# The first block of a transformer layer: first modulation sum on TensorE, the later ones in pairs on VectorE, with fixed orders

## The chip, the cores and the metric

The kernel runs on one core of one Trainium2 chip. The metric is the device time of one execution in microseconds (us): 996.87 is the median of three runs of the kernel before (996.62 to 997.46). The core has a matrix engine (TensorE, PE), VectorE (DVE), ScalarE (ACT), GpSimd (POOL), and SyncE (SP), whose queue issues nearly all loads. Each engine works through its own list of instructions in order, and waits on semaphores for the others. Sums on the matrix engine are built in PSUM, which the kernel uses as eight buffers of 128 x 512 float32.

## The reference, cut to what matters

One layer on a sequence of 512 tokens with 1024 features. The change concerns its beginning, which normalizes the input, modulates it by a condition c, and multiplies it by w_in:

```
c_act = silu(c)
mod = c_act @ w_ada + b_ada                      # (6 * 1024)
sh_t, sc_t, gt_t, sh_f, sc_f, gt_f = split(mod, 6)
h = layer_norm(x) * (1 + sc_t) + sh_t            # (512, 1024)
p = h @ w_in                                     # the first columns here, more later
```

A rotary table, cos and sin of pos * freqs, is computed beside it. Pooling, latent attention, spatial gating, an output projection and a feed-forward part with a short convolution follow; the change leaves them alone.

## The kernel before, in words

Every product is made of three: each factor is split into a high part (float32r) and a rest (low), and hi*hi, hi*lo and lo*hi are added up in PSUM.

The head, from the start to the first gate of its own (tile pg), computes 704 columns of h @ w_in: 448 latent columns into four buffers (lat, one for each 128 tokens), and 256 gate columns into two (g0ps). It walks over the 1024 features in eight pieces j of 128, and each piece has this work:

- loads on SP's queue (first_loads, L238): four tiles ada of 128 x 512 with the weights of this piece's shift and scale, and the piece's rows of w_in in two parts (w0);
- the modulation sum (first_modulation, L247): eight blocks of 128 features of c, 256 columns each, weighted by c_act on DVE in eight operations and added up into acc (two halves of four blocks each);
- prepare (L388): ACT rounds w0 to its high part w0h, POOL subtracts for the low part w0l; four one-column matmuls (L403) with a vector of ones add acc over the partitions into pm, ACT adds the bias (md, L409); four transposes turn x (pt, L414); ACT scales and shifts pt to hTjh and, once more in full precision, hfull (L420, L421), POOL subtracts for hTjl (L422);
- first_columns (L427): twelve products into lat, and first_gates (L437): six into g0ps.

x is normalized first: statistics on DVE (x_stats), an inverse root on POOL (power), and scaling on ACT (x_norm). Three wide matmuls (warm, L305) on normalized x run ahead of the first sum. The angles of the rotary table are made on DVE at the start (angles), reduced in two rounds between the sums (reduce_angles, L207), and turned to sines on ACT (sines, L217), in the program's text behind the sum of the last piece. Two gates with their own weights wg (gate, L354) follow the head: load, wsplit on ACT and DVE (L86), 24 products each (L111 to L114).

The order on each engine is made by a scheduler from the program's text and its data; `tc.issue_after(ins)` keeps what is inside it behind an instruction in this order, without a wait on the chip. So the orders below are those of the built program. SP's queue has eight loads open at a time: each load's issue waits for the landing of the load eight places before it, ACT's three loads of constants (kst, posi, cols; cols holds c, the biases and other columns) counted in.

Of the kernel before, what the change touches and what calls it, by code (L numbers as in the profile page):

```python
# [15 lines left out]
P = 128  # L16
# [34 lines left out]
def trunk(ctx: ExitStack, tc: tile.TileContext, A, out):  # L51
# [74 lines left out]
    def power(dst, src, scale, eps, n):  # L126
# [4 lines left out]
        nc.gpsimd.tensor_tensor(out=dst, in0=t[:, :n], in1=neghalf[:, :n], op=ALU.pow)  # L131
# [31 lines left out]

    kst = const.tile([P, N_CONST], F32, name="kst")
    nc.scalar.dma_start(out=kst, in_=A["consts"])
    posi = const.tile([P, TT], I32, name="posi")
    nc.scalar.dma_start(out=posi, in_=A["pos"])
    cols = const.tile([P, N_COLS], F32, name="cols")
    nc.scalar.dma_start(out=cols, in_=A["cols"])
# [29 lines left out]
    def angles():  # L199
        posf = const.tile([P, TT], F32, name="posf")  # L200
        nc.vector.tensor_copy(out=posf, in_=posi)
        for t in range(TT):
            nc.vector.tensor_scalar_mul(
                out=ang[:, t, :], in0=kst[:, K_FREQ : K_FREQ + 32], scalar1=posf[:, t : t + 1]
            )

    def reduce_angles(step):  # L207
# [4 lines left out]
        for c2 in TWO_PI:  # L212
            nc.vector.scalar_tensor_tensor(
                out=ang, in0=kq, scalar=-c2, in1=ang, op0=ALU.mult, op1=ALU.add
            )

# [15 lines left out]
    angles()  # L232

    first_raw = {}
    first_acc = {}
    last_acc = []

    def first_loads(j):  # L238
        ada = [act_t(f"ada{j}_{q}", F32) for q in range(4)]
        for q in range(4):  # L240
            nc.sync.dma_start(out=ada[q], in_=A["ada1"][j, q])
        raw = [act_t(f"w0{j}{i}", F32) for i in range(2)]
        nc.sync.dma_start(out=raw[0][:, :NL], in_=A["w0"][j, :, :NL])
        nc.sync.dma_start(out=raw[1][:, :256], in_=A["w0"][j, :, NL:])
        return ada, raw

    def first_modulation(j):  # L247
        adas, first_raw[j] = loads.pop(j)
        acct = act_t(f"acc{j}", F32)
        acc = [acct[:, :256], acct[:, 256:]]  # L250
        with ExitStack() as order:
            for ins in last_acc:
                order.enter_context(tc.issue_after(ins))
            for q in range(4):
                ada = adas[q]
                for i in range(2):
                    k = 2 * q + i
                    src = ada[:, i * 256 : (i + 1) * 256]
                    if q == 0:
                        nc.vector.tensor_scalar_mul(out=acc[i], in0=src, scalar1=cact[:, k : k + 1])  # L260
                    else:
                        ins = nc.vector.scalar_tensor_tensor(
                            out=acc[i], in0=src, scalar=cact[:, k : k + 1], in1=acc[i],
                            op0=ALU.mult, op1=ALU.add,
                        )
        last_acc[:] = [ins.ins]
        first_acc[j] = acc

    loads = {j: first_loads(j) for j in range(2)}


# [9 lines left out]
    def x_scales(a, b):  # L281
        power(rsx[:, a:b, 0], mvx[:, a:b, 1], 1.0, LN_EPS, b - a)
        nc.vector.scalar_tensor_tensor(
# [4 lines left out]
    def x_norm(t, n):  # L288
        nc.scalar.activation(
            xs[t][n], xs[t][n], AF.Identity, bias=rsx[:, t, 1:2], scale=rsx[:, t, 0:1]  # L290
        )

    for t in range(TT):
        stats = x_stats(t)
        if t % 2:
            x_scales(t - 1, t + 1)
            for u in (t - 1, t):
                x_norm(u, 0)
    first_modulation(0)
    first_modulation(1)  # L300

    warm = ps("warm")

    for t in (0, 0, 1):
        nc.tensor.matmul(warm, ident, xs[t][0], start=True, stop=True)  # L305
# [7 lines left out]
    def late_norm():  # L313
        with after_split():
            for t in range(TT):
                x_norm(t, 1)
# [69 lines left out]
    split_done = []  # L386

    def prepare(j):  # L388
        raws = first_raw[j]
        acc = first_acc[j]  # L390
# [9 lines left out]
        pm = ps("pm")  # L400
        for i in range(2):
# [1026 lines left out]
```

## Time and profile before

| What | Value |
|---|---|
| median of three runs | 996.87 us (996.62 to 997.46) |
| the profiled execution, its own time | 998.22 us |
| its span, first to last instruction | 996.1 us |
| PE busy over the span | 962.3 us (97%) |
| first product of the head (L433) | 19.17 us after the start |
| first pg, the end of the head (L111) | 69.26 us |
| mean granted clock of PE | 0.988 |

The profile's rows read: start in us, duration in us, engine, line, operation, output<-inputs, shape and a count; in square brackets the idle time of the engine just before and who ended it. Rows of adjacent instructions of one line are merged (x4). A float32 matmul shows as two rows (passes), one of float32r or a transpose as one. Rows by stretch of time give, for each engine, the busy us and a count, then the clock granted to PE (1.00 is full), the share of the DMA engines in use, and GB/s. A row of waits says which engine and line waited for whom: total us, times, longest.

### The profile page before, as it was taken

Reading aid. Unit: us, or ns where it says so; the run is one execution under the profiler, and the core shown is the slowest. Engines: PE = TensorE matmul, PEld = TensorE weight load, DVE = VectorE, ACT = ScalarE, POOL = GpSimd, SP = SyncE. Lnnn points to the kernel's source line nnn. Section 1 sums busy time; section 2 is a strip of 40 time slices with the busy share of each in tenths; the row PEclk is TensorE's granted clock in tenths of the full one; section 3 lists DMA queues with packets and bytes.
Section 4 is the critical chain, followed back from the end, with each engine's and each line's share of the span. In section 5 each row is a group of like instructions: output and inputs, shape, how many; then the busy total and the mean of one; then the engine's idle time right before and its main releaser. Section 6 shows DMA issues by size and latency. Waiting matters only on the chain.

```text
span 996.1 us, 12225 instructions
## 1 busy us (share of the span) xinstructions
PE 962.3 (97%) x4530; PEld 801.6 (80%) x4530; DVE 595.4 (60%) x923; ACT 392.7 (39%) x656; POOL 310.5 (31%) x311
## 2 busy tenths in 40 slices
PE   4999999999999999999999998999999999999996
PEld 3878888888878888888888876898888888888885
DVE  6937666566676565565433477685655565732357
ACT  3555555543233322422332244554444444422121
POOL 3556110222350022200011756421111121666654
PEclk9989999999999999999999998999999999999999
DMA  9703111125444633363223272133333343343222
GB/s 341 267 30 96 48 59 52 57 100 175 132 133 159 202 125 92 110 225 117 82 85 105 84 243 97 43 107 127 112 120 125 108 137 96 96 137 106 85 85 84
DMA packets 45274, 119.18 MB, mean 120 GB/s; under 512 B 5280, under 2 KB 8736, under 8 KB 45216
## 3 DMA queue, kind: packets, MB, share of 16 engines
q1 hardware_dynamic: 44784, 118.25, 36.4%
q8 instruction: 35, 0.57, 0.2%
q10 hardware_dynamic: 432, 0.17, 0.1%
q14 instruction: 23, 0.19, 0.1%
HBM read 116.30 MB, written 2.10 MB: 119 GB/s over the span
## 4 chain that ended last, share of the span: by engine, by line
PE 82%; DMA 6%; DVE 5%; POOL 3%; issue 2%; ACT 1%; DVEq 0%; POOLq 0%; SPq 0%; ACTq 0%
PE pzu L112 7%; PE pzu L111 7%; PE pzu L114 7%; PE pg L111 4%; PE pg L112 4%; PE pg L114 4%; PE py L111 4%; PE py L114 4%; PE py L112 4%; PE pyd L1045 3%; PE pyd L1042 3%; PE pyd L1044 3%; PE pu L848 3%; PE pu L847 3%; PE pu L845 3%
## 5 line engine op out<-in xcount | busy, mean ns | idle before, releaser
L91 DVE TENSOR_TENSOR wupl<-wup,wuph 128x1024 fp32r<-128x1024 f32 x38 | 48.8, 1285 | 71.4 <-PE pzu L114 45.6
L1011 POOL TENSOR_TENSOR d<-d,gtfb 128x512 f32<-128x512 f32 x44 | 75.3, 1732 | 34.5 <-DMA d<-in_wdn 32.0
L1284 POOL TENSOR_TENSOR zc<-zc 128x512 f32<-128x512 f32 x22 | 29.7, 1349 | 175.4 <-ACT zc L1283 154.6
L378 POOL TENSOR_TENSOR mg<-mg,th 128x512 f32<-128x512 f32 x16 | 31.3, 1959 | 146.0 <-DVE th L375 146.0
L1016 DVE TENSOR_TENSOR dl<-d,dh 128x1024 fp32r<-128x1024 f32 x18 | 29.7, 1649 | 54.5 <-PE pyd L1042 51.2
L90 ACT CAST wuph<-wup 128x1024 fp32r<-128x1024 f32 x38 | 39.9, 1050 | 46.5 <-PE pzu L112 46.5
L91 DVE TENSOR_TENSOR wgl<-wg,wgh 128x1024 fp32r<-128x1024 f32 x22 | 26.9, 1222 | 49.3 <-ACT wgh L90 36.5
L90 ACT CAST wbh<-wb 128x1024 fp32r<-128x1024 f32 x24 | 25.2, 1050 | 71.2 <-PE py L112 54.3
L725 DVE SCALAR_TENSOR_TENSOR ada<-adar,cact,ada 128x512 f32<-128x512 f32 x56 | 49.8, 917 | 0.6 <-DMA adar<-in_ada 0.5
L1015 ACT CAST dh<-d 128x1024 fp32r<-128x1024 f32 x18 | 18.9, 1052 | 61.2 <-PE pyd L1045 37.2
L1266 ACT ACTIVATE zc<-pzu,cols 128x512 f32<-128x512 f32 x44 | 34.2, 779 | 21.6 <-PE pzu L114 16.9
L90 ACT CAST wgh<-wg 128x1024 fp32r<-128x1024 f32 x22 | 23.3, 1060 | 41.6 <-PE pg L112 26.4
L91 DVE TENSOR_TENSOR wsgl<-wsg,wsgh 128x1024 fp32r<-128x1024 f32 x16 | 19.6, 1225 | 32.2 <-ACT wsgh L90 26.4
L91 DVE TENSOR_TENSOR wbl<-wb,wbh 128x1024 fp32r<-128x1024 f32 x24 | 31.1, 1294 | 9.9 <-ACT wbh L90 5.5
L90 ACT CAST wsgh<-wsg 128x1024 fp32r<-128x1024 f32 x16 | 16.8, 1052 | 49.0 <-PE pu L848 44.3
L1269 DVE SCALAR_TENSOR_TENSOR zc<-pzu,cols,zc 128x511 f32<-128x511 f32 x44 | 32.6, 743 | 3.9 <-ACT zc L1266 3.9
L646 POOL TENSOR_SCALAR pe<-pe,mx 128x128 f32<-128x128 f32 (+3 forms) x32 | 17.0, 533 | 54.4 <-DVE mx L645 54.0
L1273 DVE SCALAR_TENSOR_TENSOR zc<-pzu,cols,zc 128x510 f32<-128x510 f32 x44 | 32.6, 745 | 0.8
L1011 POOL TENSOR_TENSOR o<-o,gttb 128x512 f32<-128x512 f32 x16 | 26.4, 1672 | 17.1 <-DMA o<-in_wo 15.5
L1283 ACT ACTIVATE zc<-zc 128x512 f32<-128x512 f32 x22 | 13.9, 631 | 42.7 <-DVE zc L1273 42.6
L375 DVE SCALAR_TENSOR_TENSOR th<-th,py 128x512 f32<-128x512 f32 x16 | 11.0, 685 | 32.7 <-PE py L114 32.7
L778 POOL TENSOR_TENSOR asum<-apad 128x527 f32<-128x527 f32 x8 | 12.2, 1522 | 56.7 <-ACT apad L773 29.8
(1423 smaller groups left out, 3176.9 us busy)
## 6 DMA issues: line engine op xcount, KB each, us to landing
wup<-in_wup SPq DMA_DIRECT2D x44, 512.0 KB, 3.6
adar<-in_ada SPq DMA_DIRECT2D x64, 256.0 KB, 3.8
wb<-in_wb SPq DMA_DIRECT2D x24, 512.0 KB, 3.6
wg<-in_wg SPq DMA_DIRECT2D x22, 512.0 KB, 3.5
d<-in_wdn SPq DMA_DIRECT2D x22, 512.0 KB, 3.5
ada<-in_ada SPq DMA_DIRECT2D x32, 256.0 KB, 5.0
wsg<-in_wsg SPq DMA_DIRECT2D x16, 512.0 KB, 3.6
wa<-in_wa SPq DMA_DIRECT2D x8, 512.0 KB, 3.6
```

Of the source, the lines that this page charges most:

```text
L90: nc.scalar.copy(out=hi[:, :n], in_=raw[:, :n])
L91: ins = nc.vector.tensor_tensor(out=lo[:, :n], in0=raw[:, :n], in1=f(hi[:, :n]), op=ALU.subtract)
L111: nc.tensor.matmul(o, wh[:, c], xl[k], start=k == 0, stop=False)
L112: nc.tensor.matmul(o, wh[:, c], xh[k], start=False, stop=False)
L114: nc.tensor.matmul(o, wl[:, c], xh[k], start=False, stop=k == KT - 1)
L378: nc.gpsimd.tensor_tensor(out=merged[m], in0=merged[m], in1=th, op=ALU.add)
L725: nc.vector.scalar_tensor_tensor(out=acc[n], in0=src, scalar=cact[:, k : k + 1], in1=acc[n], op0=ALU.mult, op1=ALU.add,)
L845: nc.tensor.matmul(pu[t], hh, wl[:, c], start=False, stop=k == KT - 1)
L1011: nc.gpsimd.tensor_tensor(out=raw[:, c], in0=raw[:, c], in1=gt[n], op=ALU.mult)
L1266: nc.scalar.activation(t, pz, AF.Identity, bias=cols[:, cc + 3 : cc + 4], scale=cols[:, cc + 2 : cc + 3])
L1269: nc.vector.scalar_tensor_tensor(out=t[:, 1:512], in0=pz[:, 0:511], scalar=cols[:, cc + 1 : cc + 2], in1=t[:, 1:512], op0=ALU.mult, op1=AL ...
L1273: nc.vector.scalar_tensor_tensor(out=t[:, 2:512], in0=pz[:, 0:510], scalar=cols[:, cc : cc + 1], in1=t[:, 2:512], op0=ALU.mult, op1=ALU.add,)
```

## The change

The order of the head's work is written out in full, and its work is dealt out anew:

- The pieces come in groups: 0, 1, and the pairs (2, 3), (4, 5), (6, 7). Pairs have a new layout of the ada weights (ada1p): eight tiles per pair, each with both pieces side by side, so that one DVE operation of 512 columns serves two pieces.
- Piece 0 isn't summed on DVE: sixteen one-column matmuls take the ada tiles as they land, with c_act as the column (raw_sums), into g0ps. Ahead of it and between its first tiles stand warm-up matmuls on cols (ten, then one and one), and one on x behind its transposes.
- Of the pair (2, 3), DVE sums six of eight rows; the last two go to PE as raw rows with c_act, four one-column matmuls more for each of the two pieces.
- Products are ordered as hi*hi, then hi*lo, for lat and g0ps; then the next piece's transposes and one-column matmuls; then lo*hi. Behind the first two, the w0 split of piece j + 2 comes after the last products of piece j.
- DVE's orders: x statistics, piece 1, the pairs, then angles and both reductions; the sines stand behind the last split. On x's third and fourth row tiles ACT first scales 128 columns only.
- All loads of the head come ahead of those for later weights (load, last_load), and ACT loads cols first, kst last.

PE at the start, before (x_76 and so on are row tiles of x, acc_174 is piece 0's sum):

```order
L305 MATMUL warm<-x_76,ident 128x512 x2
L305 MATMUL warm<-x_78,ident 128x512
L403 MATMUL pm<-ones,acc_174 128x1
L414 MATMUL pt<-ident,x_76 128x128
L414 MATMUL pt<-ident,x_78 128x128
L414 MATMUL pt<-ident,x_80 128x128
L414 MATMUL pt<-ident,x_82 128x128
L403 MATMUL pm<-ones,acc_174 128x1 x3
L433 MATMUL lat_196<-w0h,hT0h 128x448
```

And now, the first seven rows, in which ada_0_114 and ada_1_115 are the first two tiles of piece 0, and lat_180 is only written to keep PE at work:

```order
L451 MATMUL lat_180<-cols,ident 128x232 x10
L442 MATMUL g0ps_181<-cact,ada_0_114 128x1
L442 MATMUL g0ps_182<-cact,ada_0_114 128x1
L442 MATMUL g0ps_181<-cact,ada_0_114 128x1
L442 MATMUL g0ps_182<-cact,ada_0_114 128x1
L451 MATMUL lat_180<-cols,ident 128x232
L442 MATMUL g0ps_181<-cact,ada_1_115 128x1
```

Nothing of DVE or of x stands ahead of the sum any more; x comes in with the transposes behind the fourth tile. The next place is PE from the transposes of one step to the next step, before:

```order
L414 MATMUL pt<-ident,x_83 128x128
L435 MATMUL lat_196<-w0h,hT5l 128x448
L435 MATMUL lat_197<-w0h,hT5l 128x448
L435 MATMUL lat_198<-w0h,hT5l 128x448
L435 MATMUL lat_199<-w0h,hT5l 128x448
L104 MATMUL g0ps_200<-hT5l,w0h 128x512
L105 MATMUL g0ps_200<-hT5h,w0l 128x512
L106 MATMUL g0ps_200<-hT5h,w0h 128x512
L104 MATMUL g0ps_201<-hT5l,w0h 128x512
L105 MATMUL g0ps_201<-hT5h,w0l 128x512
L106 MATMUL g0ps_201<-hT5h,w0h 128x512
L403 MATMUL pm<-ones,acc_570 128x1 x4
```

And now, where acc_328 holds the sums of pieces 6 and 7:

```order
L459 MATMUL pt<-ident,x_83 128x128
L475 MATMUL pm<-ones,acc_328 128x1 x2
L508 MATMUL lat_177<-w0h,hT5l 128x448
L508 MATMUL lat_178<-w0h,hT5l 128x448
L508 MATMUL lat_179<-w0h,hT5l 128x448
L508 MATMUL lat_180<-w0h,hT5l 128x448
L513 MATMUL g0ps_181<-hT5l,w0h 128x512
L513 MATMUL g0ps_182<-hT5l,w0h 128x512
L508 MATMUL lat_177<-w0h,hT6h 128x448
```

Before, pm at the end of step 5 was that of piece 7, a step ahead; now it is that of piece 6, needed by the very next step, and six products lie between it and hT6h. Two matmuls serve it in place of four. Third, DVE from the sum of piece 6 to the angles, before:

```order
L260 TENSOR_SCALAR acc_506<-ada_0_494,cact 128x256 x2
L262 SCALAR_TENSOR_TENSOR acc_506<-ada_1_495,cact,acc_506 128x256 x2
L262 SCALAR_TENSOR_TENSOR acc_506<-ada_2_496,cact,acc_506 128x256 x2
L262 SCALAR_TENSOR_TENSOR acc_506<-ada_3_497,cact,acc_506 128x256 x2
L260 TENSOR_SCALAR acc_570<-ada_0_558,cact 128x256 x2
L262 SCALAR_TENSOR_TENSOR acc_570<-ada_1_559,cact,acc_570 128x256 x2
L262 SCALAR_TENSOR_TENSOR acc_570<-ada_2_560,cact,acc_570 128x256 x2
L262 SCALAR_TENSOR_TENSOR acc_570<-ada_3_561,cact,acc_570 128x256 x2
L208 TENSOR_SCALAR kq<-ang 128x128
```

And now:

```order
L291 TENSOR_SCALAR acc_328<-ada_0_288,cact 128x512
L293 SCALAR_TENSOR_TENSOR acc_328<-ada_1_289,cact,acc_328 128x512
L293 SCALAR_TENSOR_TENSOR acc_328<-ada_2_290,cact,acc_328 128x512
L293 SCALAR_TENSOR_TENSOR acc_328<-ada_3_291,cact,acc_328 128x512
L293 SCALAR_TENSOR_TENSOR acc_328<-ada_4_292,cact,acc_328 128x512
L293 SCALAR_TENSOR_TENSOR acc_328<-ada_5_293,cact,acc_328 128x512
L293 SCALAR_TENSOR_TENSOR acc_328<-ada_6_294,cact,acc_328 128x512
L293 SCALAR_TENSOR_TENSOR acc_328<-ada_7_295,cact,acc_328 128x512
L205 CAST posf<-posi 128x4
```

Eight operations of 512 columns stand where sixteen of 256 stood, and all work on angles is behind them. On ACT, the two sine operations moved from ahead of hT6h to behind hT7h and its copy, ahead of the first wgh cast; on SP, the two wg and the wqr load moved from behind piece 1's loads to behind piece 7's.

The diff, cut to its core:

```
 def load(src, n, name):
-        nc.sync.dma_start(out=raw[:, :n], in_=src)
+        with tc.issue_after(last_load[0]):
+            nc.sync.dma_start(out=raw[:, :n], in_=src)
...
+    GROUPS = ((0,), (1,), (2, 3), (4, 5), (6, 7))
+    RAW = (6, 7)
+    def first_modulation(g, k0=0, k1=KT):
...
+        for k in range(k0, k1):
+            if len(js) == 1:
+                src = adas[k // 2][:, (k % 2) * 256 : (k % 2 + 1) * 256]
+                acc = first_acc[js[0]][k % 2]
+            else:
+                src = adas[k]
+                acc = first_sum[g]
...
+    def raw_sums(q):
+        for k in (2 * q, 2 * q + 1):
+            for i in range(2):
+                o = (k % 2) * 256 + i * P
+                ins = nc.tensor.matmul(
+                    g0psum[i][:, 0:1], first_ada[0][q][:, o : o + P], cact[:, k : k + 1],
+                    start=k == 0, stop=k == KT - 1,
+                )
+        return ins
+    def warm_up(n, src):
+        for _ in range(n):
+            w = src.shape[1]
+            ins = nc.tensor.matmul(lat[3][:, :w], ident, src, start=True, stop=True)
+        return ins
...
+            for i in range(2):
+                parts = [(part, ones[:, 0:1]) for part in acc]
+                if j in GROUPS[2]:
+                    o = (j - GROUPS[2][0]) * 256
+                    parts += [(first_ada[2][k][:, o : o + 256], cact[:, k : k + 1]) for k in RAW]
...
+        else:
+            sums = [g0psum[i][:, 0:1] for i in range(2)]
+            on_tensor(warm_up, 10, cols[:, :232])
+            for q in range(4):
+                on_tensor(raw_sums, q)
+                if q < 2:
+                    on_tensor(warm_up, 1, cols[:, :232])
+            on_tensor(turn)
...
+    first_split(0)
+    prepare(0)
+    on_tensor(warm_up, 1, xs[1][0])
+    late_norm((2, 3), 0, P)
+    first_split(1)
+    for g in range(2, len(GROUPS)):
+        first_loads(g)
+    behind = (
+        (first_modulation, 2, 0, RAW[0]), (first_modulation, 3, 0, 4), (first_modulation, 3, 4),
+        (first_modulation, 4, 0, 4), (first_modulation, 4, 4),
+        (angles,), (reduce_angles, COARSE), (reduce_angles, 1.0),
+    )
+    for work in behind:
+        on_vector(*work)
     for j in range(KT):
         hh, hl = hT_hi[j], hT_lo[j]
         wh, wl = w0s[j]
+        on_tensor(first_products, j, (hh, hh), (wh, wl), j == 0, False)
+        if j + 1 < KT:
+            on_tensor(prepare, j + 1)
+        if j < 2:
+            late_norm((2 * j, 2 * j + 1), 1, 0)
+        on_tensor(first_products, j, (hl,), (wh,), False, j == KT - 1)
+        if j + 2 < KT:
+            first_split(j + 2)
+    with after_split():
+        sines()
```

on_vector and on_tensor run a piece of work behind the one before it on their engine, by issue_after; first_products is the former twelve and six products in the order told above.

More of the change, by code (lines that the diff above doesn't have):

```diff
@@ L236, in trunk @@
     last_acc = []
[L238 to L250, printed above, removed]
+    last_load = []
@@ L251, in first_modulation, with on_vector @@
+    def on_vector(work, *args):
         with ExitStack() as order:
-            for ins in last_acc:
+            for ins in vector_last:
                 order.enter_context(tc.issue_after(ins))
[L254 to L265, printed above, removed]
@@ L286, in x_scales, with x_norm, x_first @@
         )
-    def x_norm(t, n):
-        nc.scalar.activation(
-            xs[t][n], xs[t][n], AF.Identity, bias=rsx[:, t, 1:2], scale=rsx[:, t, 0:1]
-        )
[L293 to L305, printed above, removed]
+    def x_norm(t, n, a=0, b=512):
+        return nc.scalar.activation(
+            xs[t][n][:, a:b], xs[t][n][:, a:b], AF.Identity, bias=rsx[:, t, 1:2], scale=rsx[:, t, 0:1]
+        )
+    def x_first(h):
+        for t in (2 * h, 2 * h + 1):
+            ins = x_norm(t, 0, 0, P if h else 512)
+        return ins.ins
+    for t in range(3):
+        on_vector(x_stats, t)
+    on_vector(x_scales, 0, 2)
+    split_done = [x_first(0)]
+    on_vector(x_stats, 3)
+    on_vector(x_scales, 2, 4)
+    x_first(1)
+    split_done.append(last_power[0])
+    on_vector(first_modulation, 1)
     def after_split():
@@ L399, in prepare, with on_tensor @@
         w0s.append((wh, wl))
-        pm = ps("pm")
-        for i in range(2):
-            for part in range(2):
-                nc.tensor.matmul(
-                    pm[:, i : i + 1], acc[part][:, i * P : (i + 1) * P], ones[:, 0:1],
-                    start=part == 0, stop=part == 1,
-                )
+    tensor_last = []
+    def on_tensor(work, *args):
+        with ExitStack() as order:
+            for ins in tensor_last:
+                order.enter_context(tc.issue_after(ins))
+            tensor_last[:] = [work(*args).ins]
@@ L409, in prepare @@
             nc.scalar.activation(
-                md[:, i : i + 1], pm[:, i : i + 1], AF.Identity, bias=bmod[:, j, i : i + 1]
-            )
-        pt = ps("pt")
-        for t in range(TT):
-            nc.tensor.transpose(
-                pt[:, t * P : (t + 1) * P], xs[t][j // 4][:, (j % 4) * P : (j % 4 + 1) * P], ident
+                md[:, i : i + 1], sums[i], AF.Identity, bias=bmod[:, j, i : i + 1]
             )
@@ L425, in prepare, with first_products @@
         hT_lo.append(hl)
-    def first_columns(j):
+        return last_matmul
+    def first_products(j, lefts, rights, start, stop):
+        for n, (hh, w) in enumerate(zip(lefts, rights)):
+            for t in range(TT):
+                ts_ = slice(t * P, (t + 1) * P)
+                nc.tensor.matmul(
+                    lat[t][:, :NL], hh[:, ts_], w[:, :NL], start=start and n == 0, stop=stop
+                )
+            for m in range(2):
+                c = slice(NL + m * P, NL + (m + 1) * P)
+                ins = nc.tensor.matmul(g0psum[m], w[:, c], hh, start=start and n == 0, stop=stop)
+        return ins
```

123 lines of the change are left out of this document (77 added, 46 removed).

## The prediction

> **What bounds the kernel now.** I read the page first, then busy time by stage, then what TensorE (PE) waited for in the head, then the clock that it was granted there, then single steps. All times are us.
>
> ```profile
> span 996.1 us, 12225 instructions
> ```
>
> The head, which the change rebuilds, is the part up to 69.26, where the first gate of the second kind (tile pg) begins. Busy time by stage, then PE's own waits up to 75:
>
> ```profile
> 0.00:11.17 11.17, 0.00 (x1) 0.00 (x1) 6.45 (x20) 2.36 (x4) 2.02 (x11) 1.00 0.81 280
> 11.17:19.17 8.00, 6.69 (x18) 3.50 (x18) 6.95 (x17) 4.17 (x9) 3.18 (x4) 1.00 1.05 394
> 19.17:69.26 50.09, 46.23 (x229) 41.37 (x229) 36.02 (x67) 25.49 (x64) 26.27 (x26) 0.86 0.49 178
> 69.26:996.14 926.88, 909.36 (x4285) 756.74 (x4283) 545.97 (x820) 360.72 (x583) 279.00 (x271) 0.99 0.35 112
> ```
>
> ```profile
> PE lat L433 <- ACT hT6h L420: 2.0, 1, 2.0
> PE pm L403 <- DVE acc L262: 1.8, 1, 1.8
> ```
>
> After 69.26 PE is busy for 909.36 of 926.88: what comes later is PE's own work, and a head that ends earlier moves it forward as a whole. In the head 19.17 pass before the first product. Then 50.09 pass for the eight steps, of which PE is busy 46.23, but at a mean clock of 0.86. Two waits make most of the idle time: 1.8 for a sum of VectorE (DVE), and 2.0 for hT6h, which stands behind the sines on ScalarE (ACT). Where the clock was lost, window by window, and how much of each window the one-column matmuls of tile pm (L403) filled, in the second fence:
>
> ```profile
> 16.60:20.00 3.40, 2.09 (x17) 1.95 (x16) 2.93 (x8) 2.07 (x5) 0.28 (x2) 1.00 1.03 408
> 20.00:23.40 3.40, 3.40 (x15) 3.20 (x14) 1.44 (x3) 0.55 (x3) 2.98 (x3) 0.50 1.04 385
> 33.70:37.10 3.40, 2.09 (x12) 1.69 (x11) 3.40 (x4) 1.85 (x6) 3.22 (x3) 1.00 1.06 382
> 54.10:57.50 3.40, 2.18 (x15) 1.84 (x13) 2.51 (x10) 1.07 (x4) 0.00 (x0) 1.00 0.00 0
> 57.50:60.90 3.40, 2.58 (x7) 2.32 (x8) 0.00 (x0) 2.51 (x7) 1.89 (x2) 0.51 0.03 5
> 60.90:64.40 3.50, 3.50 (x13) 3.04 (x12) 0.00 (x0) 1.45 (x2) 1.43 (x3) 0.50 0.00 0
> ```
>
> ```profile
> 16.60:20.00 3.40, 0.92 (x8) 0.86 (x7) 1.00 1.03 408
> 20.00:23.40 3.40, 1.70 (x8) 1.95 (x8) 0.50 1.04 385
> 54.10:57.50 3.40, 0.95 (x8) 1.05 (x8) 1.00 0.00 0
> ```
>
> The clock falls to 0.50 at 20.0 and at 57.5, after windows with 2.09 and 2.18 busy, but it holds after one with 2.09 busy (33.7 to 37.1). Without pm the three are 1.17, 1.23 and 2.09: one-column matmuls don't keep the clock. Nor do they bring it back: 20.0 to 23.4 is full, half of it with pm, and stays at 0.50. It came back at 26.8 and 64.4, each time after a window full of other matmuls. The two spells last 6.8 each and cost half of what PE does in them: 3.4 for the first, and 3.0 for the second, as PE restarts only at 58.3.
>
> **One step before, and what it costs after.** PE from step 4 to step 5, at full clock:
>
> ```profile
> 45.81 0.45 PE L433 MATMUL lat<-w0h,hT4h 128*128 128x448 f32 x1
> 47.53 0.60 PE L414 MATMUL pt<-ident,x 128*128 128x128 f32 x4
> 47.89 1.06 PE L435 MATMUL lat<-w0h,hT4l 128*128 128x448 f32 x4
> 48.78 0.40 PE L104 MATMUL g0ps<-hT4l,w0h 128*128 128x512 f32 x1
> 50.17 0.95 PE L403 MATMUL pm<-ones,acc 128*128 128x1 f32 x8
> 50.97 0.45 PE L433 MATMUL lat<-w0h,hT5h 128*128 128x448 f32 x1
> ```
>
> From start to start: eight products 1.72, four transposes 0.36, four products 0.89, six gate products 1.39, eight passes of pm 0.80, or 0.1 each. That is 3.95 to 4.0 of products per step, which the change orders anew and keeps. Its pm passes: 8 for piece 1 (two halves, two columns), 12 each for pieces 2 and 3 (a sum and two raw rows), 4 each for 4 to 7: 48 passes, 4.8. Before, the seven pieces after the first took 56, 5.6.
>
> The products with hTl now cover the way from pm over md to the next hTh. How long that way is shows the start of the head:
>
> ```profile
> 11.17 5.49 PE L305 MATMUL warm<-x,ident 128*128 128x512 f32 x6 [11.17 <-ACT x L289]
> 17.13 0.73 PE L403 MATMUL pm<-ones,acc 128*128 128x1 f32 x6
> 17.89 0.41 ACT L409 ACTIVATE md<-pm,bmod 128x1 f32<-128x1 f32 x2 [3.20 <-PE pm L403]
> 18.34 0.78 ACT L420 ACTIVATE hT0h<-pt,md 128x512 fp32r<-128x512 f32 x1
> 19.17 0.47 PE L433 MATMUL lat<-w0h,hT0h 128*128 128x448 f32 x1 [1.31 <-ACT hT0h L420]
> ```
>
> From the end of pm (17.86) to the first product (19.17) 1.31 pass, and pm ends about 0.15 after the next matmul could start (its last pass is 0.25 long, they follow at 0.1): 1.46. The cover is four products and two gate products, 0.89 + 0.46 = 1.35. So each step gains a new wait of 0.1; seven of them, 0.8. Sum for the steps: 8 × 3.95 + 7 × 0.36 + 4.8 + 0.8 = 39.7 against 50.1, so **−10.4**, with the clock at full rate.
>
> **The start.** The first sum no longer passes through DVE. What it then waits for are its four tiles, cols, and PE's own warm-up. The rows are the loads of constants, and SP's issues; each issue waits for the landing of the load eight places ahead, so they tell when earlier tiles had landed:
>
> ```profile
> 0.79 0.41 ACTq L165 DMA_DIRECT2D kst<-in_consts  x1
> cols<-in_cols ACTq DMA_DIRECT2D x1, 117.5 KB, 4.7
> kst<-in_consts ACTq DMA_DIRECT2D x1, 48.0 KB, 3.2
> 10.08 1.68 SPq L241 DMA_DIRECT2D ada<-in_ada  x3
> 12.78 0.33 SPq L244 DMA_DIRECT2D w<-in_w  x1
> 17.44 0.43 SPq L243 DMA_DIRECT2D w<-in_w  x1
> ```
>
> Cols is now issued at 0.79, and lands between 4.0 (with kst's 3.2) and 5.5 (with its own 4.7, for 117.5 KB); I take 4.8, nearer to its own row. The change orders the rest: ten warm-ups of 232 columns. A 512-column pass took 0.86 in the row of warm (six in 5.49, the tail included), so 232 columns take 0.39, and a warm-up of two passes 0.78, at the low rate; pm's passes went from 0.2 to 0.1 with the clock, so I take half of it, 0.39, once the clock is granted. Windows of 3.4 leave a grant between 8.2 and 11.6, in this profile's phase at 9.8: 6.4 warm-ups by then, the rest by 11.2. Then come four batches of 8 passes (0.8 each) and two warm-ups between them (0.39 each): 15.2. The second tile of piece 0 had landed by 11.4 (last of the three issues at 10.08), the fourth by 12.78, so PE sets this end. With 0.15, then md, hT0h and their gaps (1.31) the first product starts at 16.6: **−2.6**. The extremes: 14.9 if the tiles alone bound it (12.78 + 0.8 + 1.31), and 18 if the clock is granted last.
>
> The window before the first product then holds one of the small warm-ups (0.36 of it), four transposes (0.36) and the last, 512 columns wide (0.85): 1.6 without one-column matmuls. That lies between the 1.23 after which the clock fell and the 2.09 after which it held. If it falls, PE works without a break at half rate for one window, and loses 1.7. Where the windows lie isn't set by the program, so I count half: **+0.8**.
>
> The Trainium skill bears on both sides of this. "TensorE: Matmul & The Clock Gate", part 1, lets the clock drop after an idle window of about 3.4 us; by it none drops here, and the sum below would be 0.8 better. This trace disagrees: it fell at 57.5 with 2.18 of 3.40 busy. The same page, part 4, has transposes not count as busy; by it the window holds 1.2 and the clock falls each time, 0.9 worse than my sum. What this trace has on that is a window later on, all at 0.50 before it and at full clock right after, of which transposes (L1141) filled 2.78:
>
> ```profile
> 617.30:620.70 3.40, 2.78 (x12) 2.38 (x12) 0.50 0.00 0
> ```
>
> So the trace disagrees here too. Transposes stay in my count.
>
> **DVE and the loads.** The pieces from 2 on are summed by operations of 512 columns, two pieces at once. Here are DVE's eight operations for one piece before, and the same operation 512 wide in a later stage:
>
> ```profile
> 48.66 0.60 DVE L260 TENSOR_SCALAR acc<-ada,cact 128x256 f32<-128x256 f32 x2
> 49.19 4.86 DVE L262 SCALAR_TENSOR_TENSOR acc<-ada,cact,acc 128x256 f32<-128x256 f32 x6
> L725 DVE SCALAR_TENSOR_TENSOR ada<-adar,cact,ada x56: 741/746/1555, 232.4 to 803.8; 128x512 f32<-128x512 f32 x56
> ```
>
> The six took 4.86, 0.8 each, beside GpSimd's (POOL's) work on the same step. For 512 columns I take 1.05, nearer to the median of 0.75 than to the longest, 1.56. Loads run at 385 GB/s (the row from 20.0), 0.68 for 256 KB. Piece 1's last tile had landed by 17.44; the first pair's eight then land at 18.1 to 22.9, the next pair's by 30.2, the last's by 37.5, with the raw weights between them, and the three gate weights, moved behind, by 43. DVE is done with the pairs at 24.4, 33.9 and 42.3. PE asks for them (steps laid end to end from 16.6) at 24.8, 36.0 and 45.6: hidden, with 0.4 to spare on the first. If each took 1.56, they would be 2.7 late and then another 1.3 and 2.9, 6.9 in all; at 1.3, midway, only the first would be, by 1.1. The angles go behind on DVE, from 42 to 48, and the sines on ACT behind hT7, where PE has 3.95 of products left; they need 0.6, the wgh cast about 1.1 more. The gate weights aren't cast before 54, so landing by 43 is no wait.
>
> **The tail.** ACT's squares of lat begin 1.8 ahead of the first pg before; now the last lat product is 1.3 ahead of it, so this chain starts 0.9 later against PE:
>
> ```profile
> 67.49 0.38 ACT L469 ACTIVATE sq<-lat 128x256 f32<-128x256 f32 x1 [0.72 <-PE lat L435]
> 76.76 0.37 ACT L475 ACTIVATE cn<-lat,rr 128x128 f32<-128x128 f32 x1 [0.95 <-POOL rr L131]
> 80.15 1.47 PE L501 MATMUL ptc<-ident,cn 128*128 128x128 f32 x12
> ```
>
> Its last cn was done at 77.1, three before PE's transposes at 80.15. For the rotary part behind it on POOL, which I have no spare time for, I put **+0.2**, between 0 and 0.9.
>
> **The sum.** −2.6 − 10.4 + 0.8 + 0.2 = −12.0. The profiled execution took 998.22, so its like would take 986.2; it stands 1.35 above the median of the runs, 996.87. From the median, 984.9.
>
> **The rivals.**
> - The clock holds in every run. For it: the window from 33.7 held it with 1.3 idle. The 0.8 goes, and the waits of 0.1 may not show: 983.3 to 984.1.
> - A new wait takes part back: DVE under POOL at 1.3 to 1.56 per operation (1.1 to 6.9), or two windows at half clock in place of one (another 1.7, as both spells before lasted two). For it: the longest L725, and 0.4 to spare on the first pair; against it, DVE's mean in the head. 986.0 to 991.8.
> - No change: the rest of the kernel gives the gain back. Against it: its 17.5 of idle time would have to grow by 12, and nothing there is tied to the time since the start. 996.9.
> - Slower: the clock stays at 0.50 through the head, because the pm passes and new waits keep any window from being full (2.58 of 3.40 didn't do, 57.5 to 60.9). All 39.7 would double: 1024. It decides from 24 at half rate on. Against it: at half rate a step has products and transposes of 5.9 without a break, longer than a window, so most steps offer one.
>
> **Chances.** Forecast 0.54 (984.1 to 986.5), clock holds 0.18, new wait 0.23, no change 0.02, slower 0.03. The range goes from 982.3 (the clock holds, and the tiles alone bound the start: 984.1 - 1.7) to 989.0, midway through the new waits; no change, slower and the far end of the waits are left out. About 0.2% (2 us) is what a measurement of this kernel can tell from no change; the first three cases are all beyond it: faster 0.95, same 0.02, slower 0.03.
>
> **What would show it.** In the profile after: the first lat product near 16.6; first pg near 56 to 58; the clock at full rate from 21 at the latest up to pg; between steps PE idle 0.1 to 0.2 with hTh as the releaser; no PE wait for acc; no pm in front of a step that stands still. Wrong would be: a PE wait for acc over 1, a clock of 0.50 after 25, or a first product after 18.

## The result, and the profile after

| | us |
|---|---|
| before, median of 4 runs beside the changed kernel | 996.75 (995.59 to 997.46) |
| changed, median of 4 runs | **990.62** (990.05 to 991.69) |
| ratio, 95% interval | 0.9943 (0.993 to 0.9955) |
| forecast | 984.9 (982.3 to 989.0) |
| profiled execution: time, span, mean clock | 991.69, 989.7, 0.993 |

The change gains 6.1 where 12.0 was forecast, and the time lies outside the range. Where TensorE (PE) waited in the head and somewhat behind it, 0 to 75 (line numbers are the changed kernel's):

```profile
PE lat L451 <- DMA cols<-in_cols: 4.5, 1, 4.5
PE pm L475 <- DVE acc L293: 2.2, 1, 2.2
```

The first row is the start, before anything can run. The second is new: the two waits of before (sines, and a sum in another place) are gone, but PE now waits 2.2 for VectorE's (DVE's) sum of the first pair, pieces 2 and 3. The same place in order of time, from piece 0's first product on:

```profile
17.37 1.08 PE L508 MATMUL lat<-w0h,hT0h 128*128 128x448 f32 x4
...
22.57 1.08 PE L508 MATMUL lat<-w0h,hT1h 128*128 128x448 f32 x4
...
25.24 0.60 PE L459 MATMUL pt<-ident,x 128*128 128x128 f32 x4
28.09 0.35 PE L475 MATMUL pm<-ones,acc 128*128 128x1 f32 x2 [2.25 <-DVE acc L293]
...
30.88 1.86 PE L508 MATMUL lat<-w0h,hT2h 128*128 128x448 f32 x4
```

Piece 0 takes 5.20 from first product to first product. Piece 1 takes 8.31, 2.25 of it the wait. Piece 2 then begins at half speed: four products in 1.86 instead of 1.08. The clock by windows of 3.41, with the part behind the head as the last row; then how much of the first window the one-column passes of pm fill:

```profile
27.42:30.83 3.41, 2.74 (x18) 2.39 (x18) 3.27 (x6) 1.20 (x4) 0.00 (x0) 1.00 1.04 370
30.83:34.24 3.41, 3.41 (x10) 2.91 (x10) 3.30 (x4) 2.83 (x5) 2.66 (x2) 0.50 1.06 373
34.24:37.66 3.42, 3.42 (x25) 3.19 (x24) 3.35 (x4) 0.68 (x3) 1.86 (x2) 1.00 1.04 383
61.83:989.70 927.87, 910.15 (x4285) 757.07 (x4283) 542.83 (x820) 361.90 (x589) 279.24 (x273) 0.99 0.35 112
```

```profile
27.42:30.83 3.41, 1.47 (x12) 1.42 (x12) 0.41 (x2) 1.00 1.04 370
```

Of 2.74 busy in the first window, 1.47 are pm; 1.27 are other matmuls, and the next window is granted 0.50. The gate's products (tile pg), the end of the head, begin at 61.83 (69.26 before, 57.1 forecast); behind it 927.87 pass, where before took 926.88.

DVE over the same time:

```profile
15.11 1.53 DVE L291 TENSOR_SCALAR acc<-ada,cact 128x256 f32<-128x256 f32 x2 [2.09 <-DMA ada<-in_ada]
16.56 3.49 DVE L293 SCALAR_TENSOR_TENSOR acc<-ada,cact,acc 128x256 f32<-128x256 f32 x6
20.08 1.24 DVE L291 TENSOR_SCALAR acc<-ada,cact 128x512 f32<-128x512 f32 x1
21.36 6.58 DVE L293 SCALAR_TENSOR_TENSOR acc<-ada,cact,acc 128x512 f32<-128x512 f32 x5
27.86 0.47 DVE L291 TENSOR_SCALAR acc<-ada,cact 128x512 f32<-128x512 f32 x1
```

Piece 1's sum occupies it until 20.05, and the first pair's six operations (the third and fourth row) then take 7.9, until 27.94; the last row already belongs to the next pair. The forecast had them begin at 18.1 and end at 24.4.

### The profile page after: what moved, and what is told of

Its sections match the earlier page's. It is cut to its first block, busy times and chain, and to the rows that moved or that the text cites. A ratio compares the mean times of both kernels' runs of the same rounds, so it can differ in the third digit from the quotient of the medians.

```text
span 989.7 us, 12259 instructions
## 1 busy us (share of the span) xinstructions
PE 965.1 (98%) x4566; PEld 804.0 (81%) x4566; DVE 590.9 (60%) x889; ACT 393.5 (40%) x658; POOL 311.1 (31%) x311
## 4 chain that ended last, share of the span: by engine, by line
PE 83%; POOL 5%; DVE 5%; DMA 4%; issue 2%; ACT 2%; DVEq 0%; SPq 0%; POOLq 0%; ACTq 0%
PE pzu L113 7%; PE pzu L112 7%; PE pzu L115 7%; PE py L112 4%; PE py L115 4%; PE py L113 4%; PE pg L112 4%; PE pg L113 4%; PE pg L115 3%; PE pyd L1128 3%; PE pyd L1125 3%; PE pyd L1127 3%; PE pu L931 3%; PE pu L930 3%; PE pu L928 3%; PE lat L508 2%
## 5 line engine op out<-in xcount | busy, mean ns | idle before, releaser
L1094 POOL TENSOR_TENSOR o<-o,gttb 128x512 f32<-128x512 f32 x16 | 26.5, 1677 | 16.6 <-DMA o<-in_wo 15.0
```

The costliest lines, as they stand in the source:

```text
L1094: nc.gpsimd.tensor_tensor(out=raw[:, c], in0=raw[:, c], in1=gt[n], op=ALU.mult)
```

## The experiments

Theory A, from these rows: the first pair's sum is late on DVE, and wait and passes together then cost a window at half clock; about 3.9 (2.25 of waiting and 1.7 of clock). The ratios below are to the kernel before, measured beside each run. Rivals: the passes drop the clock whatever DVE does (B), what the head gains is given back behind it (C), the loss lies in the start.

**Fewer rows on DVE.**

```
-    RAW = (6, 7)
+    RAW = (4, 5, 6, 7)
```

> Theory A (the first pair's sum on VectorE ends late, TensorE waits 2.25 for it, and the window with that wait brings a stretch of 3.41 at half clock that costs 1.7): with four of the eight rows on TensorE, VectorE has two operations of 1.3 less and ends at 25.3, before TensorE asks at 25.8. The wait goes (-2.2), the half clock goes (-1.7), 16 more one-column passes cost 1.6: 988.3. Rival B (the one-column passes themselves drop the clock, the wait does not): the wait goes, the half clock stays, 16 passes are paid: 990.0. Rival C (what is gained there is given back behind the head): the head is 2.3 shorter, the time stays at 990.6.

990.35 (989.29 to 992.61, 6 runs), ratio 0.9937 (0.9924 to 0.9949). The wait is gone, and yet the clock fell at 30.49. The windows, then pm's part in the second and the fourth:

```profile
27.08:30.49 3.41, 3.41 (x29) 3.24 (x26) 3.30 (x4) 0.99 (x3) 1.52 (x2) 1.00 0.99 365
30.49:33.90 3.41, 3.41 (x10) 2.75 (x9) 3.30 (x4) 3.04 (x6) 1.89 (x2) 0.50 1.06 369
33.90:37.30 3.40, 3.40 (x28) 3.22 (x28) 3.33 (x4) 0.00 (x0) 1.68 (x2) 1.00 1.00 358
```

```profile
27.08:30.49 3.41, 2.29 (x20) 2.27 (x20) 0.41 (x2) 1.00 0.99 365
33.90:37.30 3.40, 2.02 (x19) 2.12 (x20) 0.00 (x0) 1.00 1.00 358
```

PE was busy for all of 27.08 to 30.49 and still lost the clock: 2.29 were one-column passes. That is B. A wait is not needed. The median fits B and C alike (990.0 and 990.6); it is the clock that decides.

**The wait filled.** Piece 2 only, ahead of its sums:

```
+            if j == 2:
+                for _ in range(5):
+                    nc.tensor.matmul(pm[:, 128:360], ident, cols[:, :232], start=True, stop=True)
```

> Five matmuls of 232 columns, whose result nothing reads, stand ahead of piece 2's sums and fill 2.0 of the 2.25 that TensorE waits there. Theory A (the wait drops the clock): no stretch of half clock at 30.8 to 34.2, so 1.7 less: 988.9, with the wait under 0.4. Rival B (the one-column passes drop it, or too few products in that window): the half clock stays, 990.6. Rival D (extra matmuls that come late hold up the sums): up to 0.5 more, 991.1.

989.8 (988.11 to 992.58, 6 runs), ratio 0.9933 (0.992 to 0.9947). No wait for pm and full clock from 18.33 through the head; the step of piece 2 takes 5.81 instead of 7.35. The gate's products are at 60.54, although this execution had lost a window at the start. With twelve passes and no idle time the clock holds, with twenty it did not. So A and B are one thing, the share of the window that is left for matmuls other than one-column passes. The time alone does not tell this run from the changed kernel: their intervals overlap.

**GpSimd's part.** The low halves of the weights of pieces 1 and 2 are left out, and the high half is multiplied in their place:

```
-                nc.gpsimd.tensor_tensor(
-                    out=wl[:, a:b], in0=raw[:, : b - a], in1=f(wh[:, a:b]), op=ALU.subtract
-                )
-        w0s.append((wh, wl))
+                if j not in (1, 2):
+                    nc.gpsimd.tensor_tensor(
+                        out=wl[:, a:b], in0=raw[:, : b - a], in1=f(wh[:, a:b]), op=ALU.subtract
+                    )
+        w0s.append((wh, wh if j in (1, 2) else wl))
```

> GpSimd's subtraction of the low half of the weights is left out for pieces 1 and 2 (two of 2.2 each); the high half is multiplied in its place, so the products have their number and shape. Theory A1 (GpSimd beside VectorE stretches VectorE's 512-wide operations from 0.75 to 1.3): the first pair ends at about 25.0, no wait of TensorE, no half clock: 990.6 - 2.2 - 1.7 = 986.7. Rival A2 (the first pair is late because it starts late, behind piece 1's sum at 20.05, or because its rows land late): its operations stay near 1.3 or wait for rows, the wait stays at 2.0 or more, 990.6.

989.02 (988.9 to 989.96, 5 runs), ratio 0.9925 (0.9913 to 0.9937). DVE's groups during the first pair's sum, in the changed kernel (20.0 to 27.9) and then here (18.1 to 23.6); the second number behind the bar is the mean of one in ns:

```profile
L293 DVE SCALAR_TENSOR_TENSOR acc<-ada,cact,acc 128x512 f32<-128x512 f32 x5 | 6.4, 1288 | 0.2
```

```profile
L293 DVE SCALAR_TENSOR_TENSOR acc<-ada,cact,acc 128x512 f32<-128x512 f32 x5 | 3.8, 752 | 0.2
```

The same five operations take 0.75 instead of 1.29 once GpSimd (POOL) does less beside them: A1. The pair is done at 23.5, 4.4 earlier. Of these, 2.5 are its own operations (7.86 before, 5.35 here). The other 1.9 are an earlier beginning, 18.15 instead of 20.08: piece 1's rows landed 0.9 earlier in this execution, and piece 1's sum, beside which GpSimd also does less, was 1.0 shorter. No wait and no half clock remain in the head, and the gate's products begin at 57.67; the forecast had 57.1. That is 4.2 earlier than in the first profile of the changed kernel. The spans of the two profiled executions differ by 2.5 (989.7 and 987.2), the medians by 1.6. So 1.6 of the 4.2 are lost again behind the head in these profiles. The waits up to 75 and PE behind the head:

```profile
PE ptk L597 <- POOL kr L575: 1.5, 1, 1.5
```

```profile
70.25 0.38 PE L601 MATMUL ptk<-ident,kr 128*64 128x128 f32 x2
72.14 0.33 PE L597 MATMUL ptk<-ident,kr 128*128 128x128 f32 x1 [1.51 <-POOL kr L575]
```

**The sines alone**, in the kernel before:

```
-                    if j + 2 == KT - 1:
-                        sines()
...
+    with after_split():
+        sines()
```

> The kernel before with one part of the change alone: the sine tables come behind the head's loop, all else as it was. If the forecast's reading of the kernel before holds (TensorE waits 2.0 at piece 7 behind ScalarE's sines and pays about 3.0 for the half clock that follows at 57.5 to 64.4): 996.75 - 5.0 = 991.8, and the stretch of half clock at 57.5 is gone. Rival: the wait goes and the clock drops all the same, because of the one-column passes: 994.7. Rival C: the sines then hold up the attention that follows and the time stays at 996.7.

994.74 (992.78 to 996.78, 12 runs), ratio 0.9981 (0.997 to 0.9992): 1.9 less, not 5. The wait of 2.0 and the half clock at 57.5 are gone, but the waits now have this, 1.8 before, and half clock follows at 39.8 for 3.41. The rival's 994.7 is met in number only, since its half clock at 57.5 is not there:

```profile
PE pm L403 <- DVE acc L262: 3.3, 1, 3.3
```

**Piece 2's columns first.** The same sum on DVE, in two column halves:

```
+                if half is not None:
+                    src = src[:, half * 256 : (half + 1) * 256]
+                    acc = acc[:, half * 256 : (half + 1) * 256]
...
-        (first_modulation, 2, 0, RAW[0]), (first_modulation, 3, 0, 4), (first_modulation, 3, 4),
+        (first_modulation, 2, 0, RAW[0], 0), (first_modulation, 2, 0, RAW[0], 1), (first_modulation, 3, 0, 4), (first_modulation, 3, 4),
```

> The changed kernel with the first pair's sum made in two column halves, piece 2's 256 columns first; TensorE's work is the same. Theory A: the six half operations for piece 2 end at 20.1 + 6 x 0.5 = 23.1, or at the last row's landing near 23, before TensorE asks at 25.2; the wait of 2.25 goes and no stretch of half clock follows it, so the first products of the gate are issued at 61.8 - 3.9 = 57.9, and the time is 990.6 - 3.9 = 986.7 if nothing behind the head is late. Theory A with the give-back that the run without GpSimd's subtractions showed (TensorE waits 1.5 for kr and loses 0.3 more): 988.5. Rival B (the one-column passes drop the clock by themselves): the wait goes, the half clock stays: 988.4 without a give-back, with the gate's products at 59.6.

992.58 (990.66 to 993.69, 5 runs), ratio 0.9964 (0.995 to 0.9977): 2.0 above the changed kernel's median, with intervals that just overlap. The wait for pm is gone and pieces 1 and 2 take 5.81 each. Against that stand kr's wait of 1.5, and two windows at half clock over the start's raw sums, so that the first product came at 19.45. None of the three forecasts had the two windows at the start.

**All rows on DVE**, on top of the halves, and then the sines behind the norms' squares as well:

```
-    RAW = (6, 7)
+    RAW = ()
```

```
+    with tc.issue_after(last_sq.ins):
+        sines()
```

> As the run with the halves, and all eight rows of the first pair on VectorE, so that TensorE has four one-column passes in place of twelve at pieces 2 and 3. Theory A: eight half operations end at 24.5, still ahead of TensorE's 25.2; 16 passes of 0.11 less, so 1.8 less than the run with the halves: the gate's products at 56.1, and 984.9 without a give-back. Rival C (the head is then shorter than what ScalarE and GpSimd need for kr): the wait for kr grows by those 1.8 to about 3.3 and the time stays at 988.5. Rival D (VectorE gets later for all pieces behind): a wait for the sums of piece 4 or 6 of up to 1, 986.

> As the run with the halves and all rows on VectorE, and ScalarE makes the sine tables behind the squares of the norms instead of ahead of them. If the give-back is that the tables, which wait for VectorE's angles, stand ahead of the squares on ScalarE: the squares start 1.2 to 1.6 earlier and the wait for kr shrinks by as much, 1.2 to 1.6 less than the run before it. If GpSimd's powers or its copies of kr beside VectorE's 1024-wide operations set it: no change beside the run before it, or up to 1 slower since the rotation then waits for the tables.

993.73 (991.83 to 995.23, 11 runs; ratio 0.9974, 0.9965 to 0.9983) and 995.69 (993.62 to 997.8, 11 runs; 0.9991, 0.9981 to 1.0002). Rival D, and larger than it said. PE's waits of the first:

```profile
PE pm L478 <- DVE acc L296: 4.4, 2, 3.3
```

The pair's sixteen half operations ended at 32.9, and half clock followed from 40.6 for 6.83. In the second the same waits are 5.4, and PE waits 1.6 for a cast that now stands behind the squares; it settles nothing about kr.

**The start without its two extra matmuls:**

```
-                if q < 2:
-                    on_tensor(warm_up, 1, cols[:, :232])
```

> The changed kernel without the two extra matmuls that stand between the raw sums of piece 0. If TensorE's own work sets the first product (the sums end at 15.8): the first product is 0.96 earlier, 16.4, and 989.6, as long as the clock holds. If the rows' landing sets it: TensorE waits for rows and the first product stays near 17.3, 990.6. If the two extra matmuls hold the clock: a stretch of half clock between 14 and 21 in most runs, 1.7 to 3.4, 991.4 to 993.

991.62 (989.27 to 993.75, 5 runs), ratio 0.9956 (0.9943 to 0.9969). The first product came at 16.36, 1.0 earlier, so PE's own work sets it in this execution. It was worth nothing: PE then stood three times before DVE's sums, half clock followed at 30.34 for 3.41, and the gate's products began at 61.42.

```profile
PE pm L475 <- DVE acc L293: 2.4, 3, 1.1
```

**Early angles**, with the halves and alone, beside the changed kernel and the halves unaltered, on one chip:

```
+    on_vector(angles)
     on_vector(x_scales, 2, 4)
...
+    on_vector(reduce_angles, COARSE)
     on_vector(first_modulation, 1)
...
-        (angles,), (reduce_angles, COARSE), (reduce_angles, 1.0),
+        (reduce_angles, 1.0),
```

> As the run with the halves, and the angles with their first reduction stand in VectorE's idle time ahead of piece 1's sum (3.2 of work at 11.6 to 15.1) instead of behind the third pair. If the give-back behind the head is ScalarE's squares, which stand behind the sine tables and so behind VectorE's angles (ready at 59.3 in the run with the halves, with the gate's products at 60.8): the angles are ready 4 to 7 earlier, the squares start 1 earlier beside the gate's products, the wait for kr falls from 1.5 to 0.5 or less, and the distance from the first transpose of kr to the first product for the queries falls from 13.9 to 12.5 to 12.9. Then the time is 1.0 to 1.4 under that of the run with the halves. If GpSimd's powers and copies alone set it: still 1.5 and 13.9, no difference. If the angles hold up piece 1's sum: a wait for it at 20, up to 1 slower.

> The changed kernel once more, unaltered, as the measure for the three beside it: 990.6, a wait for the first pair's sum of 2.25 give or take 0.5 and a stretch of half clock in the head within the two windows behind it, if these belong to the kernel; without both, if they belonged to the one execution shown.

> The run with the halves once more, unaltered. Its first profile had two windows of half clock over the start's sums, which the changed kernel's had not, and the first product 2.1 later. If that belongs to the execution, not to the kernel: a first product at 17.4 or less, the gate's products at 57.9, and a time of 988.5 to 990. If it belongs to the kernel: 992.5 again, with half clock at the start in the profile again.

> The changed kernel with the angles and their first reduction ahead of piece 1's sum, nothing else. If the wait for the first pair is VectorE held up by GpSimd: it stays at 2.25 and the head as it is; behind the head kr's wait of 0.2 goes: 990.4. If the angles push piece 1's sum and the pairs: a wait of 2.5 to 4, 991 to 992.5.

| run | median (range) | ratio, interval | half clock at the start | wait for pm | gate's products |
|---|---|---|---|---|---|
| halves, early angles | 991.42 (989.76 to 992.36) | 0.9946 (0.9931 to 0.996) | 3.41 | none | 58.73 |
| changed, again | 990.32 (989.02 to 992.33) | 0.9939 (0.9923 to 0.9955) | none | 1.4 | 58.94 |
| halves, again | 991.92 (990.84 to 992.74) | 0.9951 (0.9937 to 0.9966) | 6.83 | none | 61.10 |
| early angles alone | 989.65 (988.07 to 991.19) | 0.993 (0.9914 to 0.9945) | 3.41 | none | 58.57 |

The changed kernel's second profile has the wait, 1.4 long, but no half clock behind it:

```profile
26.72 0.35 PE L475 MATMUL pm<-ones,acc 128*128 128x1 f32 x2 [1.40 <-DVE acc L293]
```

So the wait belongs to the kernel, and the half clock does not come with it every time: it depends on how long the wait is and on how the windows lie. The waits for kr are 0.2 in all four profiles, those of the halves unaltered included, which had 1.5 in their first profile. So early angles took no wait away here, and of the 1.0 to 1.4 expected from them with the halves 0.5 is in the medians, within their intervals. The halves' start was as before; here are its windows:

```profile
11.69:15.10 3.41, 3.29 (x27) 3.30 (x27) 0.40 (x3) 1.64 (x4) 1.02 (x3) 1.00 1.03 370
15.10:18.50 3.40, 3.40 (x16) 3.26 (x16) 3.08 (x7) 0.80 (x4) 1.74 (x2) 0.50 0.99 333
18.50:21.90 3.40, 3.40 (x8) 2.19 (x7) 3.25 (x7) 3.23 (x6) 1.97 (x2) 0.50 0.99 363
```

Of the 14 profiles of the changed kernel and its variants, five show no half clock at the start, six one window, three two. The first product of piece 1 came at 22.06 without (changed, again), 23.36 after one (the filled wait) and 25.85 after two (halves, again): 1.3 and 3.8 later. Where the start is slow, DVE gains on PE, and the wait goes: early angles alone show no wait. There PE asks 0.8 later than in the first profile of the changed kernel, and the pair also takes 6.5 instead of 7.9, with POOL busy for 3.6 of it instead of 5.5.

The three profiles with two windows have one thing in common that the other eleven have not. PE waits over 1 for a tile of piece 0 ahead of its first raw sums (halves, halves again, and the last version below; 0.6 at most in the others):

```profile
PE g0ps L445 <- DMA ada<-in_ada: 1.5, 1, 1.5
PE g0ps L445 <- DMA ada<-in_ada: 1.3, 1, 1.3
PE g0ps L444 <- DMA ada<-in_ada: 1.4, 1, 1.4
```

So in these executions the landing of the rows holds up the start, and the late sums reach into a second window. That one causes the other is not shown. Why the tile was late in both of the halves' profiles, and why their times are some 1.5 above the changed kernel's, stays open.

**Without the subtractions, and angles early; and the version that seemed best** (early angles, and three instead of five matmuls to fill the wait). They put together edits shown above.

> GpSimd's low halves of the weights left out for pieces 1 and 2 as before (the high half is multiplied in their place), and the angles with their first reduction ahead of piece 1's sum. If kr's wait of 1.5 came from the angles at the end of VectorE's queue: the wait falls to 0.2, the distance from the first transpose of kr to the first product for the queries from 13.9 to 12.5, the gate's products stay at 57.7, and the time is 989.0 - 1.4 = 987.6. If kr's wait is GpSimd's and VectorE's own work behind the head: 13.9 again and 989.0.

> The changed kernel with early angles and three matmuls of 232 columns ahead of piece 2's sums, which fill 1.2 of the wait for the first pair. If fill and early angles add: 989.65 (early angles alone) less 0.5 to 1.0 for the windows of half clock that the fill saves in part of the executions: 988.9. If early angles had already taken the wait away: the fill only costs, up to 1.2: 990.5.

989.62 (987.92 to 990.73, 5 runs; ratio 0.9932, 0.9919 to 0.9945) and 991.51 (989.09 to 992.66, 6 runs; 0.9947, 0.9933 to 0.9961). Without the subtractions, kr's wait is now this:

```profile
PE ptk L599 <- POOL kr L577: 0.2, 1, 0.2
```

That comes from ScalarE (ACT): kr stands on POOL behind the powers of the norms, which wait for ACT's squares (sq). First the run with the angles last, then with early angles:

```profile
55.77 0.31 ACT L227 ACTIVATE sinT<-ang 128x128 f32<-128x128 f32 x1 [1.58 <-DVE ang L224]
...
57.93 0.36 ACT L553 ACTIVATE sq<-lat 128x256 f32<-128x256 f32 x1
```

```profile
54.91 0.30 ACT L227 ACTIVATE sinT<-ang 128x128 f32<-128x128 f32 x1
...
57.46 0.39 ACT L555 ACTIVATE sq<-lat 128x256 f32<-128x256 f32 x1 [0.70 <-PE lat L511]
```

With the angles last, the sines wait for DVE and hold up the squares, which start 0.26 behind the gate's first product (57.67); with early angles the squares wait for nothing but PE and start 0.87 ahead of it (58.33). So kr's wait of 1.5 comes from the squares' being late, here by the angles' place. The halves show the same without any edit: their squares started 0.14 behind the gate's first product in the first profile (60.90 and 60.76; wait 1.5) and 0.86 ahead of it in the second (60.24 and 61.10; wait 0.2). The profiled execution took 987.92, near the 987.6 expected and the lowest of its five, although it had lost a window at the start. The median did not follow (989.0, then 989.6); why is not shown. The last version's profile lost two windows; its time is above both expectations, 988.9 and 990.5. No variant that computes everything can be told from the changed kernel on the faster side; early angles alone come nearest.

## Why the prediction was wrong

**The step that failed** is DVE's: "DVE is done with the pairs at 24.4, 33.9 and 42.3 ... hidden, with 0.4 to spare on the first." The first pair ended at 27.9. Of the 3.5, 2.0 are the beginning: the sum was let start with its landings at 18.1, while DVE was on piece 1 until 20.05. The other 1.5 are the price of one operation, 1.3 in place of 1.05. PE asked at 25.8 instead of 24.8, so 2.25 of waiting were left of the 3.5. The 1.05 was put between the median and the longest of a later stage of the kernel before. But an operation takes 0.75 alone, and longer by what POOL does at that moment. Three rows of the changed kernel show it:

```profile
25.13 1.13 POOL L425 TENSOR_TENSOR w0l<-w,w0h 128x448 fp32r<-128x448 f32 x1 [0.57 <-ACT w0h L424]
25.14 1.67 DVE L293 SCALAR_TENSOR_TENSOR acc<-ada,cact,acc 128x512 f32<-128x512 f32 x1
...
36.42 0.75 DVE L293 SCALAR_TENSOR_TENSOR acc<-ada,cact,acc 128x512 f32<-128x512 f32 x1
```

The DVE operation at 25.14 begins just behind POOL's and ends at 26.81, 0.55 after POOL's has ended (26.26). The one at 36.42 has no POOL operation beside it. The first pair is summed where POOL (5.43 in the row below) is at work for most of the time:

```profile
20.05:27.90 7.85, 5.79 (x35) 4.84 (x33) 7.64 (x7) 4.03 (x8) 5.43 (x5) 1.00 1.05 378
```

Five operations at 0.75 and one of 0.47 are 4.2. The whole took 7.85, so 3.6 of POOL's 5.43 were added. The Trainium skill states the mechanism ("SBUF — State Buffer", section "Who interferes with whom"): a VectorE instruction with two SBUF inputs and a GpSimd instruction that reads SBUF exclude each other, and the later one stands until the other is through. The trace agrees: 0.752 against 1.288 for the same five. An estimate by that page is between 4.2 and 9.6 for the pair, the latter with the 5.43 added in full. The forecast had 6.3, with 0.4 to spare. Its rival "a new wait" had the mechanism and a price of 986.0 to 991.8, in which the measured time lies, at a chance of 0.23. But at 1.3 per operation it had a wait of 1.1, where it was 2.25 and 1.4 in the two profiles, because it too let the sum begin at 18.1. Two of the forecast's three signs of being wrong came in the first profile: a wait for acc over 1, and a clock of 0.50 after 25.

**The clock behind that wait** (1.7 in one profile, none in the other) had no step. The forecast's own reading, that one-column passes do not keep the clock, would have given it: a wait of 2.25 and passes of 1.3 (28.09 to 29.42) exceed a window of 3.41.

**The start** was right in kind: the first product came at 17.37 and 16.86, 16.6 forecast; the run without the extra matmuls shows that PE sets it there; in three profiles a tile's landing did. Its clock term, 0.8 for half a window lost, was too small: over the 14 profiles (6 × 1.3 + 3 × 3.8)/14 is about 1.4, since two windows in a row can go.

**The steps** were right. PE per step with nothing late:

```profile
48.07 1.08 PE L508 MATMUL lat<-w0h,hT5h 128*128 128x448 f32 x4
...
51.16 0.51 PE L475 MATMUL pm<-ones,acc 128*128 128x1 f32 x4
...
52.98 0.88 PE L508 MATMUL lat<-w0h,hT6h 128*128 128x448 f32 x3
```

4.91, against 3.95 + 0.36 + 0.4 + 0.1 = 4.8. In the run without the subtractions, which has no wait and no half clock in the head, all steps together took 40.6 (17.06 to 57.67), 39.7 forecast, and the head ended 0.6 later than forecast.

**The tail** was put at +0.2. It is +1.0 in the first profile (927.87 against 926.88) and +2.7 in the second (988.5 - 58.94 = 929.56). Counted from the gate's first product and against the kernel before, PE is 0.4 late at the last transposes of kr in both profiles, and another 1.0 and 1.4 late once the queries have their last weight (wqk). From 577 on the first profile gets 0.4 back and the second loses 0.9 more; what does that was not followed up. The angles ran from 43.9 to 57 on DVE, not "from 42 to 48". With the heads of these two profiles that left kr's wait at 0.2; a head of the forecast's length would have paid 1.5, if it goes as in the run without the subtractions. As for the queries' weight, SP's issue of its load, in the changed kernel and in the filled one:

```profile
121.89 1.07 SPq L682 DMA_DIRECT2D wqk<-in_wqk  x1
```

```profile
120.56 0.38 SPq L685 DMA_DIRECT2D wqk<-in_wqk  x1
```

ACT's cast then waits for it (first row), and in the second profile of the changed kernel PE waits for the cast:

```profile
125.98 0.51 ACT L685 CAST wqk3h<-wqk 128x384 fp32r<-128x384 f32 x1 [1.01 <-DMA wqk<-in_wqk]
```

```profile
PE pqn L105 <- ACT wqk3h L685: 0.5, 1, 0.5
```

What holds the issue was not tried, and an issue as short as the second is followed by a longer wait in another run (2.1 before the same cast, all rows on DVE). So the claim that a head that ends earlier moves the rest forward as a whole held but for 1 to 2.7.

**The sum.** Over the two profiles of the changed kernel the head ended 3.3 later than forecast (60.4 against 57.1), and what follows lost 1.7 more than the 0.2 allowed: 5.0 of the 5.7 between 984.9 and 990.6. The remaining 0.7 is within what executions differ by. Two bounds of the range are off by 0.1 in the forecast's own terms: 984.1 - 1.7 is 982.4, and midway between 986.0 and 991.8 is 988.9.

**The sines** were read from the rows of before as a wait of 2.0 and a half clock of 3.0. Moved alone they are worth 1.9, since DVE's sum was next in line, with a wait of 3.3 in place of 1.8 and a new loss of clock.

## What to carry to other kernels

Price an operation of VectorE by its time alone and by what GpSimd runs at that moment, and not as a mean over a stage: here the sum lay between its time alone and that plus all of GpSimd's. Let it begin when its data are there and what stands ahead of it in its own queue is done as well. When work is put last on a queue, lay its whole length against the new, shorter schedule, since its reader may be behind the stage that gains. And a gain in one place is worth only the distance to what is next in line: here the start, the sum and the clock each hid behind one another.

## What the runs showed of the hardware

The clock falls with a window's lack of matmuls other than one-column passes, not with idle time. Without these passes, windows with 1.12 (fewer rows on DVE) and 1.27 (the changed kernel) of 3.41 lost it, the first with PE busy throughout. One with 1.38 (33.90 to 37.30 of the run with fewer rows, 3.40 - 2.02) held it: the clock is full from 33.9 to the end of the head. So did one with PE idle for 1.57 and no such passes (24.00 to 27.41 of the changed kernel). In all sixteen profiles, up to 75, the 18 windows behind which the clock fell have 1.27 at most, and those behind which it stayed full have 1.37 at least. The Trainium skill ("TensorE: Matmul & The Clock Gate", part 1) has the windows run free of the program, about 3.4 long: the trace agrees, with 3.413 and another position in each execution. Its condition, a window without activity, the trace doesn't bear out.

Runs of one kernel differ by 1 to 4.7 us, about the size of the effects in question; windows of 1.7 each, lost in some executions only, are part of that. A single profile shows one draw.
